# The expert layer of a two-layer block: the last 64 of 256 tokens by gathered expert rows, and the gates' one-hot rows by one comparison and ScalarE

## The chip, the cores and the metric

One core of a Trainium2 chip runs the whole program. The metric is device time in microseconds (us), the median of three runs; the profile shows one execution.

## The reference

256 tokens of width 2048 pass through a first layer (a convolution and a state-space branch, then a layer of experts) and a second one (a delta-rule block and a banded attention). The change touches the experts only: 16,384 experts of one neuron each, of which every token picks 128 (8 heads, 16 each).

```python
def block(xb):                       # PEER_TOKEN_BLOCK = 128 tokens; 8 heads, 2 x 128 keys
    q = (xb @ w_q).reshape(PEER_TOKEN_BLOCK, PEER_HEADS, 2, PEER_HALF)
    s = jnp.einsum('thcd,hcnd->thcn', q, sub_keys).astype(jnp.float32)
    s_top, i_top = lax.top_k(s, PEER_TOPK)
    cand = s_top[:, :, 0, :, None] + s_top[:, :, 1, None, :]
    cand_idx = i_top[:, :, 0, :, None] * PEER_KEYS + i_top[:, :, 1, None, :]
    ...
    best, pos = lax.top_k(cand, PEER_TOPK)
    expert = jnp.take_along_axis(cand_idx, pos, axis=-1)
    gates = jax.nn.softmax(best, axis=-1).astype(xb.dtype)
    u_sel = u_tab[expert]
    v_sel = v_tab[expert]
    act = jax.nn.gelu(jnp.einsum('td,thkd->thk', xb, u_sel))
    return jnp.einsum('thk,thkd->td', gates * act, v_sel)
```

## The kernel before

The kernel reads no expert row by its index. It computes all 16,384 activations of all 256 tokens and multiplies them by a dense matrix of gates, which is zero where an expert is not picked.

Every matrix product is made of split operands. A piece of weights of 128 x 1024 (512 KB) is fetched into one of three buffers `raw` (L150, the SP queue); ScalarE casts it to a rounded high part `wh` (L162), VectorE subtracts that from it and leaves the low part `wl` (L163). `wh` and `wl` are rings of 2048 columns. `self.width` says how many columns one cast and one subtraction take: 1024 (W1) in the mixers, 512 (W2) from the experts on. Both are put ahead of other work in the engines' programs (`high_priority`). The activations stand in the same two parts beside each other, so `dual` makes a product from two instructions: `wh` on both parts (512 columns, L175) and `wl` on the high part (256 columns, L176). `fold` adds the two halves of the result (ScalarE L181, VectorE L182).

The expert layer runs in this order:

- **Queries** (`experts_in`): 16 blocks of 16 products each with `peer_w_q`; each block's scores against the sub-keys go into a table, and VectorE picks the top 16 of them by `topk`, in small steps that are laid between the products (`Side`, `TSTEP` steps a block). These steps reach into the next stage.
- **peer_u**: 128 blocks, block c giving expert activations for all tokens: 16 products, `fold`, a scaling by `rstd` (L797), a gelu into `w` (L801). From c = 31 on, when the top-k is done, `gates` runs beside the products, `GRATE` steps for each product: for each token three VectorE comparisons with a counting row (L942, L944) make a one-hot row of the first key scaled by the gate's power of two, and two of the second key scaled by the gate's high and low part. After eight tokens 16 products (L954) give a 128 x 128 block of gates for each of them, and `gate_block` multiplies it into `w` (VectorE L966) where block c is done, or copies it there (ScalarE L968) where it is not. For tokens whose gates are there when a block is finished, gelu and gate are multiplied at once (L803, L804).
- **peer_v** (`experts_out`): `w` is the stationary operand now. It is split again, 128 experts x 256 tokens at a time (ScalarE L1009, VectorE L1010), and for each of the two halves of the tokens three products of 512 columns (L1018 to L1020) are added in PSUM. Three groups of 512 output columns are summed in one pass over the experts, the fourth in a second pass, beside which the first three are finished: transposed, added to the residual and prepared for the second layer (`finish`, `take_x2`).

Each engine works through its instructions in the order of its program.

Of the kernel before, what the change touches and what calls it, by code (L numbers as in the profile page):

```python
# [10 lines left out]
F32 = mybir.dt.float32  # L11
# [11 lines left out]
P = 128  # L23
W1 = 1024
W2 = 512
STEP = (6, 2, 2.25, 3.7, 3, 2)
GRATE = 0.2
# [18 lines left out]
KT = 16  # L46
MAGIC = 1.5 * 2.0**23
# [68 lines left out]

class K:
# [54 lines left out]
    def dual(self, pf, wh, wl, hl, start, stop):  # L172

        nc = self.nc
        nc.tensor.matmul(pf, lhsT=wh, rhs=hl, start=start, stop=False)  # L175
        return nc.tensor.matmul(pf[:, :T], lhsT=wl, rhs=hl[:, 0], start=False, stop=stop)  # L176

    def fold(self, pf):

        t = self.foldp.tile([P, T], F32, name="fold")[: pf.shape[0]]  # L180
        self.nc.scalar.copy(t, pf[:, T:])  # L181
        self.nc.vector.tensor_tensor(out=pf[:, :T], in0=pf[:, :T], in1=t, op=ALU.add)  # L182
        return pf[:, :T]

    def gemm_steps(self, ps, pieces, x):

        last = 8 * len(pieces) - 1
        k = 0
        for src in pieces:
            for wh, wl in self.load_split(src):  # L190
                self.marks["P"] = self.dual(ps, wh, wl, x.hl[:, k], k == 0, k == last)
                k += 1
                if k > last:
                    self.fold(ps)
                yield

    def gemm(self, pieces, x, between=None):
        pf = self.gps_tile()
        for _ in self.gemm_steps(pf, pieces, x):
            if between is not None:  # L200
                next(between, None)
        return pf[:, :T]
# [68 lines left out]
    def first(self):  # L271
        tc = self.tc
        self.width = W1
        with ExitStack() as ctx:
# [3 lines left out]
            with ExitStack() as c2:  # L278
# [6 lines left out]
                self.width = W2  # L285
                self.em = Tmp(E(tc.tile_pool(name="em", bufs=8)))
# [455 lines left out]
    def experts_in(self):  # L742
# [3 lines left out]
        with ExitStack() as ctx:  # L746
# [6 lines left out]
            ijg = c2.tile([P, 5, T], F32, name="ijg")  # L753
# [11 lines left out]
            nc.gpsimd.tensor_copy(iota16, iota)  # L765
            tk = self.topk(sc, bt, ijg, iota)
            def score(k, q):
# [8 lines left out]
            for k in range(16):  # L776
# [8 lines left out]
                side.step(TSTEP, (self, "V"))  # L785
            score(15, q)
            side.add(tk(8))

            w = [self.big_tile("w0").rearrange("p (c t) -> p c t", c=32)]
            tokens = Side()  # L790
            self.gated = 0

            for c in range(P):
                self.block = c
                ps = self.gemm([I["peer_u"][c, 0], I["peer_u"][c, 1]], x, self.mix((tokens, GRATE, "")))
                g = sm.tile([P, T], F32, name="gg")
                V.tensor_tensor(out=g, in0=ps, in1=rstd, op=ALU.mult)  # L797
                d = self.expert(w, c)
                n = self.gated
                if n < T:  # L800
# [5 lines left out]
                if c == 31:  # L806
                    side.drain()
                    w += [self.big_tile(f"w{k}").rearrange("p (c t) -> p c t", c=32) for k in (1, 2)]
                    w += [self.half_tile(f"w{k}").rearrange("p (c t) -> p c t", c=16) for k in (3, 4)]
                    tokens.add(self.gates(wps, ijg, iota16, w))  # L810
            assert not tokens.q
            self.w = w

    def expert(self, w, c):
        return w[c // 32][:, c % 32, :] if c < 96 else w[3 + (c - 96) // 16][:, c % 16, :]

    def topk(self, sc, bt, ijg, iota):
# [54 lines left out]
        def last():  # L872
# [39 lines left out]
            ij = ij.rearrange("p c h e k -> p c h (e k)")  # L912
            for h in range(2):
                for k, src in enumerate((ij[:, 0, h, :], ij[:, 1, h, :], ex.rearrange("p g k -> p (g k)")[:, h * P : h * P + P])):
                    pt = self.ips.tile([P, 512], F32, name="pt", tag="i")[:, :P]
                    nc.tensor.transpose(pt, src, self.ident)
                    nc.scalar.copy(ijg[:, k, h * P : h * P + P], pt)
# [5 lines left out]
            half = area(128).bitcast(F16)  # L923
# [7 lines left out]
    def gates(self, wps, ijg, iota, w):  # L931
# [6 lines left out]
        for t in range(T + GLAG):  # L938
            if t < T:
                oj = self.em.tile([P, 3, P], F16, name="oj")  # L940
                oi = oj[:, 2, :].bitcast(BF16)
                V.tensor_scalar(out=oi, in0=iota, scalar1=ijg[:, 0, t : t + 1], scalar2=ijg[:, 4, t : t + 1], op0=ALU.is_equal, op1=ALU.mult)  # L942
                for k in range(2):
# [822 lines left out]
```

## Time and profile before

| | |
|---|---|
| median of 3 runs | 3355.83 us (3353.45 to 3359.02) |
| the profiled execution's own time | 3351.08 us |
| its span, first to last instruction | 3349.3 us |
| mean granted TensorE clock | 0.996 of full speed |
| busy share: TensorE, VectorE, ScalarE, GpSimd | 98%, 80%, 60%, 5% |
| bytes moved | 584.49 MB, 175 GB/s on average |

A row of the trace gives an instruction's duration from its start to its end. Instructions of one engine can overlap, so a sum of durations can exceed the engine's busy time; TensorE's overlap most, and their pace is read from the starts. "DMA share" is the mean busy share of the core's 16 DMA engines.

### The profile page before, as it was taken

The numbers are of one execution on the slowest core, as the hardware profiler recorded it, in microseconds if no ns is written. First come the engines' busy times: TensorE is split into PE (matmuls) and PEld (weight loads), VectorE is DVE, ScalarE is ACT, GpSimd is POOL, SyncE is SP. The second block draws the span as 40 slices with busy tenths as digits, with TensorE's granted clock in tenths as the row PEclk, the third lists the DMA queues.
The fourth block names the chain that finished last, engine by engine and source line by source line (L and its number), as shares of the span: only waits on it lengthen the run. The fifth ranks groups of instructions, "written<-read, shape, count | busy, mean of one in ns | idle before, by whom it ended". The sixth has DMA issues, their size and how long they took to land.

```text
span 3349.3 us, 53879 instructions
## 1 busy us (share of the span) xinstructions
PE 3291.0 (98%) x17962; PEld 2780.5 (83%) x17962; DVE 2667.1 (80%) x6200; ACT 2021.3 (60%) x4529; POOL 171.6 (5%) x319
## 2 busy tenths in 40 slices
PE   8999999999999999999999999999999999999999
PEld 7787778888888888888888888778888888888888
DVE  8999987789999999996555556868888768666685
ACT  6577755555555555555555556767666666566664
POOL 1211110000000000000000000000222100000000
PEclk9999999999999999999999999999999999999999
DMA  6544345765556555555666666655443436655556
GB/s 210 160 143 139 133 127 188 216 193 178 187 183 179 180 177 182 177 182 183 193 194 195 193 192 198 209 183 171 143 138 117 145 105 211 198 177 176 173 171 181
DMA packets 167655, 584.49 MB, mean 175 GB/s; under 512 B 19184, under 2 KB 25616, under 8 KB 167120
## 3 DMA queue, kind: packets, MB, share of 16 engines
q1 hardware_dynamic: 165600, 574.94, 54.8%
q0 software_dynamic: 1776, 6.10, 0.6%
q8 instruction: 141, 2.31, 0.3%
q14 instruction: 138, 1.13, 0.1%
HBM read 573.88 MB, written 7.09 MB: 173 GB/s over the span
## 4 chain that ended last, share of the span: by engine, by line
PE 90%; DVE 5%; ACT 2%; issue 1%; DMA 1%; POOL 1%; SPq 0%; ACTq 0%; DVEq 0%; POOLq 0%
PE g L175 36%; PE g L176 18%; PE va L1018 7%; PE va L1019 7%; PE va L1020 7%; PE g L1609 3%; PE g L1610 3%; PE g L1608 3%; DVE wl L163 2%; PE ip L1345 1%; ACT wh L162 1%; PE yp L639 1%; PE wp L954 1%; PE cps L175 1%; PE bu L611 1%
## 5 line engine op out<-in xcount | busy, mean ns | idle before, releaser
L162 ACT CAST wh<-raw 128x512 fp32r<-128x512 f32 (+1 forms) x1920 | 1274.2, 664 | 1080.3 <-PE g L175 553.2
L163 DVE TENSOR_TENSOR wl<-raw,wh 128x512 fp32r<-128x512 f32 (+1 forms) x1920 | 1433.8, 748 | 589.6 <-ACT wh L162 571.8
L175 PE MATMUL g<-X,wh 128*128 128x512 f32 x4752 | 1707.7, 401 | 23.0 <-ACT wh L162 8.8
L176 PE MATMUL g<-X,wl 128*128 128x256 f32 x4752 | 1337.0, 281 | 2.3 <-DVE wl L163 2.2
L175 PEld LDWEIGHTS g<-X,wh 128*128 128x128 f32 x4752 | 894.3, 188 | 234.6 <-issue 10.8
L176 PEld LDWEIGHTS g<-X,wl 128*128 128x128 f32 x4752 | 898.0, 189 | 9.9 <-DVE wl L163 5.1
L1018 PE MATMUL va<-wh,ah 128*128 128x512 f32 x1024 | 398.4, 391 | 4.5 <-DVE gg L797 2.3
L1019 PE MATMUL va<-wh,al 128*128 128x512 f32 x1024 | 400.2, 391 | 0.3 <-DVE al L1010 0.3
L1020 PE MATMUL va<-wl,ah 128*128 128x512 f32 x1024 | 399.1, 390 | 0.0
L1018 PEld LDWEIGHTS va<-wh,ah 128*128 128x128 f32 x1024 | 191.7, 188 | 46.9 <-ACT ah L1009 7.5
L1019 PEld LDWEIGHTS va<-wh,al 128*128 128x128 f32 x1024 | 192.6, 188 | 43.3 <-DVE al L1010 3.3
L1020 PEld LDWEIGHTS va<-wl,ah 128*128 128x128 f32 x1024 | 192.7, 188 | 39.7
L175 PE MATMUL g<-xo,wh 128*128 128x512 f32 x512 | 179.6, 395 | 0.0
L182 DVE TENSOR_TENSOR g<-g,fold 128x256 f32<-128x256 f32 x377 | 159.8, 424 | 4.5 <-ACT fold L181 4.0
L1608 PE MATMUL g<-wh,X 128*128 128x512 f32 x384 | 151.9, 396 | 0.0
L1610 PE MATMUL g<-wl,X 128*128 128x512 f32 x384 | 150.5, 392 | 0.0
L1609 PE MATMUL g<-wh,X 128*128 128x512 f32 x384 | 150.1, 391 | 0.0
L181 ACT COPY fold<-g 128x256 f32<-128x256 f32 x377 | 138.2, 367 | 13.5 <-DVE g L182 7.7
L176 PE MATMUL g<-xo,wl 128*128 128x256 f32 x512 | 143.6, 280 | 0.0
L944 DVE TENSOR_SCALAR oj<-iota,ijg 128x128 f16<-128x128 f16 x512 | 142.6, 307 | 0.0
L175 PEld LDWEIGHTS g<-xo,wh 128*128 128x128 f32 x512 | 96.0, 187 | 22.8 <-DVE xo L1471 0.3
L1010 DVE TENSOR_TENSOR al<-w,ah 128x256 fp32r<-128x256 f32 x256 | 106.7, 418 | 0.9 <-ACT ah L1009 0.8
(478 smaller groups left out, 3577.0 us busy)
## 6 DMA issues: line engine op xcount, KB each, us to landing
raw<-peer_u SPq DMA_DIRECT2D x256, 512.0 KB, 3.5
raw<-peer_v SPq DMA_DIRECT2D x256, 512.0 KB, 3.5
raw<-a_w_in SPq DMA_DIRECT2D x128, 512.0 KB, 3.5
raw<-w_in SPq DMA_DIRECT2D x112, 512.0 KB, 3.5
raw<-b_w_t SPq DMA_DIRECT2D x96, 512.0 KB, 3.5
raw<-w_out SPq DMA_DIRECT2D x32, 512.0 KB, 4.3
raw<-peer_w_q SPq DMA_DIRECT2D x32, 512.0 KB, 3.5
raw<-a_w_out SPq DMA_DIRECT2D x32, 512.0 KB, 3.7
```

Of the source, the lines that this page charges most:

```text
L162: self.marks["A"] = nc.scalar.copy(wh[:, e], raw[:, e])
L163: self.marks["V"] = nc.vector.tensor_tensor(out=wl[:, e], in0=raw[:, e], in1=wh[:, e].bitcast(F32), op=ALU.subtract)
L175: nc.tensor.matmul(pf, lhsT=wh, rhs=hl, start=start, stop=False)
L176: return nc.tensor.matmul(pf[:, :T], lhsT=wl, rhs=hl[:, 0], start=False, stop=stop)
L182: self.nc.vector.tensor_tensor(out=pf[:, :T], in0=pf[:, :T], in1=t, op=ALU.add)
L944: V.tensor_scalar(out=oj[:, k, :], in0=iota, scalar1=ijg[:, 1, t : t + 1], scalar2=ijg[:, 2 + k, t : t + 1], op0=ALU.is_equal, op1=ALU.mult)
L1018: nc.tensor.matmul(ps, lhsT=ah, rhs=wh, start=first, stop=False)
L1019: nc.tensor.matmul(ps, lhsT=al, rhs=wh, start=False, stop=False)
L1020: nc.tensor.matmul(ps, lhsT=ah, rhs=wl, start=False, stop=last)
L1608: nc.tensor.matmul(ps[a], lhsT=xh[:, k, s], rhs=wh, start=k == 0, stop=False)
L1609: nc.tensor.matmul(ps[a], lhsT=xl[:, k, s], rhs=wh, start=False, stop=False)
L1610: self.marks["P"] = nc.tensor.matmul(ps[a], lhsT=xh[:, k, s], rhs=wl, start=False, stop=k == KT - 1)
```

## The change

The last 64 tokens (S) no longer take part in the products of peer_u: those, the one-hot rows and the gates are made for 192 tokens (N). For the 64, a class `Picks` holds the picked experts' numbers and gates with one row for each token and half of its 128 picks. Gather c brings pick c of each row, 128 expert rows, into one of two buffers by an indirect DMA from GpSimd's queue. In peer_u there are 64 gathers of rows of 2048 elements (8 KB each), and one VectorE instruction for each multiplies the rows by the tokens and sums them (`dots`, two steps for three blocks, from c = 32 on). In peer_v there are 64 gathers of 1536 and then 64 of 512 elements, and VectorE adds each, times its coefficient, to a sum (`sums`, one step for two blocks); `finish` folds the two rows of a token by a product with `sel`. In peer_v the first operand now has tokens 64 to 191 and needs three products as before; the second has the high and low part of tokens 0 to 63 side by side and needs two.

The one-hot rows of two tokens are made by one VectorE comparison of 512 elements, and ScalarE scales them by the gates in six instructions of 128 elements. `self.width` is not lowered to 512 any more, the pool `em` has 7 buffers in place of 8, `w` lies in blocks of 42, and `GRATE` goes from 0.2 to 0.08, each step now being two tokens. Three copies of the expert tables in row order are added to the kernel's inputs.

```diff
-GRATE = 0.2
+GRATE = 0.08
+S = 64
+N = T - S
+NW = 8192 // N
+USTEP = 2.0 / 3.0
...
+class Picks:
...
+    def rows(self, x, rstd):
+        k, nc = self.k, self.k.nc
+        xs = self.buf[0].rearrange("p (k i t) -> p k i t", k=KT, i=2)
+        h, l = (v.bitcast(F32)[:, :, N:].unsqueeze(2).to_broadcast([P, KT, 2, S]) for v in x)
+        nc.vector.tensor_tensor(out=xs, in0=h, in1=l, op=ALU.add)
+        r = rstd[:, N:].unsqueeze(1).unsqueeze(1).to_broadcast([P, KT, 2, S])
+        nc.vector.tensor_tensor(out=xs, in0=xs, in1=r, op=ALU.mult)
...
+                nc.tensor.transpose(ps[:, i * P : i * P + P], xs[:, 4 * q + i, :], k.ident)
+            nc.scalar.copy(self.acc[:, 512 * q : 512 * q + 512], ps)
...
+    def gather(self, table, c, w):
+        b = self.buf[c % 2][:, :w]
+        off = bass.IndirectOffsetOnAxis(ap=self.idx[:, c : c + 1], axis=0)
+        self.k.nc.gpsimd.indirect_dma_start(out=b, out_offset=None, in_=table, in_offset=off)
+        return b
+    def stream(self, table, w, use):
+        bufs = [self.gather(table, c, w) for c in range(2)]
+        yield
+        for c in range(S):
+            use(c, bufs[c % 2])
+            if c + 2 < S:
+                self.gather(table, c + 2, w)
+            yield
+    def dots(self):
...
+            V.tensor_tensor_reduce(out=b, in0=b, in1=self.acc, scale=1.0, scalar=0.0, op0=ALU.mult, op1=ALU.add, accum_out=self.h[:, c : c + 1])
...
+    def sums(self, table, o, w):
...
+                V.scalar_tensor_tensor(out=acc, in0=b, scalar=s, in1=acc, op0=ALU.mult, op1=ALU.add)
...
     def dual(self, pf, wh, wl, hl, start, stop):
...
+        n = hl.shape[2]
+        nc.tensor.matmul(pf[:, : 2 * n], lhsT=wh, rhs=hl, start=start, stop=False)
+        return nc.tensor.matmul(pf[:, :n], lhsT=wl, rhs=hl[:, 0], start=False, stop=stop)
...
-                self.width = W2
-                self.em = Tmp(E(tc.tile_pool(name="em", bufs=8)))
+                self.em = Tmp(E(tc.tile_pool(name="em", bufs=7)))
...
+                if k == 1:
+                    self.picks.rows(x, rstd)
...
-                ps = self.gemm([I["peer_u"][c, 0], I["peer_u"][c, 1]], x, self.mix((tokens, GRATE, "")))
+                ps = self.gemm([I["peer_u"][c, 0], I["peer_u"][c, 1]], x, self.mix((tokens, GRATE, ""), (sparse, USTEP / 16, "")), N)
...
+            sparse.drain()
...
-                V.tensor_scalar(out=oi, in0=iota, scalar1=ijg[:, 0, t : t + 1], scalar2=ijg[:, 4, t : t + 1], op0=ALU.is_equal, op1=ALU.mult)
-                for k in range(2):
-                    V.tensor_scalar(out=oj[:, k, :], in0=iota, scalar1=ijg[:, 1, t : t + 1], scalar2=ijg[:, 2 + k, t : t + 1], op0=ALU.is_equal, op1=ALU.mult)
+        for t in range(0, N + GLAG, 2):
...
+                V.tensor_tensor(out=oj[:, :, 0::2, :], in0=iota.unsqueeze(1).unsqueeze(1).to_broadcast([P, 2, 2, P]),
+                                in1=self.ij16[:, t : t + 2, :].unsqueeze(3).to_broadcast([P, 2, 2, P]), op=ALU.is_equal)
+                for i in range(2):
+                    c = slice(t + i, t + i + 1)
+                    oi = oj[:, i, 0, :]
+                    nc.scalar.activation(oi.bitcast(BF16), oi, AF.Copy, scale=ijg[:, 4, c])
+                    nc.scalar.activation(oj[:, i, 1, :], oj[:, i, 2, :], AF.Copy, scale=ijg[:, 3, c])
+                    nc.scalar.activation(oj[:, i, 2, :], oj[:, i, 2, :], AF.Copy, scale=ijg[:, 2, c])
...
+                        pa = self.em.tile([P, 2 * N + S], F32R, name=f"pa{e}")
+                            nc.scalar.copy(pa[:, :N], a)
+                            nc.scalar.copy(pa[:, N:T], a[:, :S])
+                            V.tensor_tensor(out=pa[:, T:], in0=a, in1=pa[:, :N].bitcast(F32), op=ALU.subtract)
+                        parts.append((pa[:, S:N], pa[:, T + S :], pa[:, N:T], pa[:, N : T + S]))
...
-                                nc.tensor.matmul(ps, lhsT=ah, rhs=wh, start=first, stop=False)
-                                nc.tensor.matmul(ps, lhsT=al, rhs=wh, start=False, stop=False)
-                                nc.tensor.matmul(ps, lhsT=ah, rhs=wl, start=False, stop=last)
+                            nc.tensor.matmul(a, lhsT=ah, rhs=wh, start=first, stop=False)
+                            nc.tensor.matmul(a, lhsT=al, rhs=wh, start=False, stop=False)
+                            nc.tensor.matmul(a, lhsT=ah, rhs=wl, start=False, stop=last)
...
+                            nc.tensor.matmul(b, lhsT=bhl, rhs=wh, start=first, stop=last)
+                            if not last:
+                                nc.tensor.matmul(b[:S], lhsT=bh, rhs=wl, start=False, stop=False)
                     side.step()
+                    sparse.step()
+                sparse.drain()
```

## Rows read from the trace of the kernel before

**Rows 1.** Windows by stage: us, busy PE PEld DVE ACT POOL, clock, DMA share, GB/s.
```profile
682.00:777.00 95.00, 95.00 (x565) 83.61 (x564) 82.89 (x264) 50.32 (x100) 0.84 (x2) 1.00 0.59 184
777.00:965.00 188.00, 188.00 (x1071) 163.16 (x1070) 178.63 (x481) 105.24 (x201) 0.00 (x0) 1.00 0.60 185
965.00:1525.00 560.00, 559.97 (x3564) 489.27 (x3563) 527.16 (x1532) 321.88 (x759) 0.00 (x0) 1.00 0.57 179
1525.00:2060.00 535.00, 532.74 (x2357) 441.15 (x2356) 316.27 (x530) 285.94 (x529) 0.00 (x0) 1.00 0.61 192
2060.00:2240.00 180.00, 177.51 (x778) 142.35 (x777) 143.90 (x292) 135.31 (x308) 2.82 (x10) 1.00 0.65 203
```

**Rows 2.** Timeline of TensorE in peer_u: start us, us, engine, line, operation.
```profile
1003.25 0.40 PE L175 MATMUL g<-X,wh 128*128 128x512 f32 x1
1003.48 0.28 PE L176 MATMUL g<-X,wl 128*128 128x256 f32 x1
1003.60 0.39 PE L175 MATMUL g<-X,wh 128*128 128x512 f32 x1
```

**Rows 3.** Timeline of TensorE in peer_v.
```profile
1700.28 0.39 PE L1018 MATMUL va<-wh,ah 128*128 128x512 f32 x1
...
1700.96 0.39 PE L1018 MATMUL va<-wh,ah 128*128 128x512 f32 x1
```

**Rows 4.** Groups of VectorE, 975 to 1520: count, busy us, mean ns, idle before.
```profile
L163 DVE TENSOR_TENSOR wl<-raw,wh 128x512 fp32r<-128x512 f32 x371 | 254.7, 686 | 21.3 <-ACT wh L162 19.7
L944 DVE TENSOR_SCALAR oj<-iota,ijg 128x128 f16<-128x128 f16 x512 | 142.6, 307 | 0.0
L942 DVE TENSOR_SCALAR oj<-iota,ijg 128x128 bf16<-128x128 f16 x256 | 78.5, 307 | 3.1 <-PE wp L954 2.8
L182 DVE TENSOR_TENSOR g<-g,fold 128x256 f32<-128x256 f32 x93 | 39.5, 424 | 0.0
L797 DVE TENSOR_TENSOR gg<-g,rstd 128x256 f32<-128x256 f32 x93 | 38.9, 419 | 2.7 <-PE wp L954 1.8
L966 DVE TENSOR_TENSOR w<-w,wp 128x256 f32<-128x256 f32 (+15 forms) x99 | 34.1, 356 | 0.0
L804 DVE TENSOR_TENSOR w<-w,gg 128x8 f32<-128x8 f32 (+31 forms) x89 | 25.5, 287 | 0.0
```

**Rows 5.** Windows, 975 to 1520 us, columns as in rows 1.
```profile
975.00:1520.00 545.00, 545.00 (x3480) 476.92 (x3479) 517.78 (x1516) 313.01 (x739) 0.00 (x0) 1.00 0.57 179
```

**Rows 6.** Groups of the whole run, shapes kept apart.
```profile
L163 DVE TENSOR_TENSOR wl<-raw,wh 128x1024 fp32r<-128x1024 f32 x192 | 238.5, 1242 | 66.4 <-ACT wh L162 66.1
L162 ACT CAST wh<-raw 128x1024 fp32r<-128x1024 f32 x192 | 201.0, 1047 | 161.6 <-PE g L175 147.0 <-issue 13.8
...
L1010 DVE TENSOR_TENSOR al<-w,ah 128x256 fp32r<-128x256 f32 x256 | 106.7, 418 | 0.9 <-ACT ah L1009 0.8
...
L674 DVE SCALAR_TENSOR_TENSOR cw<-cw 128x256 f32<-128x256 f32 x150 | 73.9, 534 | 0.0
```

**Rows 7.** Windows, 200 to 300 us, in the mixers, columns as in rows 1.
```profile
200.00:300.00 100.00, 98.42 (x536) 81.08 (x534) 99.91 (x181) 75.56 (x173) 10.31 (x12) 1.00 0.44 144
```

**Rows 8.** Timeline, two ScalarE scalings by a column of scales.
```profile
701.54 0.69 ACT L248 ACTIVATE dg<-ident,r_yi 128x128 f32<-128x128 f32 x2
```

**Rows 9.** Windows, 2294 to 2302 us, columns as in rows 1.
```profile
2294.00:2302.00 8.00, 8.00 (x48) 6.97 (x47) 6.71 (x16) 3.79 (x8) 0.20 (x2) 1.00 0.95 357
```

**Rows 10.** Timelines of GpSimd and VectorE, near 2291 and near 2388 us.
```profile
2291.53 0.56 POOL L1191 DMA_DIRECT2D rep<-gd  x1 [0.35 <-issue]
...
2291.99 0.69 DVE L163 TENSOR_TENSOR wl<-raw,wh 128x512 fp32r<-128x512 f32 x1 [0.69 <-ACT wh L162]
...
2388.18 3.81 POOL L1337 TENSOR_TENSOR xx<-tab 128x2048 f32<-128x2048 f32 x1 [2.92 <-DMA tab<-xdr]
...
2388.71 3.43 DVE L1268 TENSOR_SCALAR ksq<-ksq 128x2 f32<-128x2 f32 x1
```

**Rows 11.** Timeline of TensorE, products of full precision.
```profile
704.29 0.71 PE L770 MATMUL pq<-bs,q 128*128 128x128 f32 x4
```

More of the change, by code (lines that the diff above doesn't have):

```diff
@@ L174, in dual, with fold, gemm_steps @@
         nc = self.nc
[L175 to L185, printed above, removed]
+        n = hl.shape[2]
+        nc.tensor.matmul(pf[:, : 2 * n], lhsT=wh, rhs=hl, start=start, stop=False)
+        return nc.tensor.matmul(pf[:, :n], lhsT=wl, rhs=hl[:, 0], start=False, stop=stop)
+    def fold(self, pf, n=T):
+        t = self.foldp.tile([P, T], F32, name="fold")[: pf.shape[0], :n]
+        self.nc.scalar.copy(t, pf[:, n : 2 * n])
+        self.nc.vector.tensor_tensor(out=pf[:, :n], in0=pf[:, :n], in1=t, op=ALU.add)
+        return pf[:, :n]
+    def gemm_steps(self, ps, pieces, x, n=T):
         last = 8 * len(pieces) - 1
@@ L794, in experts_in @@
                 self.block = c
-                ps = self.gemm([I["peer_u"][c, 0], I["peer_u"][c, 1]], x, self.mix((tokens, GRATE, "")))
-                g = sm.tile([P, T], F32, name="gg")
-                V.tensor_tensor(out=g, in0=ps, in1=rstd, op=ALU.mult)
+                ps = self.gemm([I["peer_u"][c, 0], I["peer_u"][c, 1]], x, self.mix((tokens, GRATE, ""), (sparse, USTEP / 16, "")), N)
+                g = sm.tile([P, N], F32, name="gg")
+                V.tensor_tensor(out=g, in0=ps, in1=rstd[:, :N], op=ALU.mult)
+                if c == 31:
+                    side.drain()
+                    w += [self.big_tile(f"w{k}")[:, : NW * N].rearrange("p (c t) -> p c t", t=N) for k in (1, 2)]
+                    w.append(self.picks.rest)
+                    tokens.add(self.gates(wps, ijg, iota16, w))
+                    sparse.add(self.picks.dots())
                 d = self.expert(w, c)
                 n = self.gated
-                if n < T:
+                if n < N:
                     nc.scalar.activation(d[:, n:], g[:, n:], AF.Gelu_apprx_tanh)
@@ L805, in experts_in @@
                 side.step(TSTEP, (self, "V"))
[L806 to L810, printed above, removed]
             assert not tokens.q
+            sparse.drain()
             self.w = w
     def expert(self, w, c):
-        return w[c // 32][:, c % 32, :] if c < 96 else w[3 + (c - 96) // 16][:, c % 16, :]
+        return w[c // NW][:, c % NW, :]
     def topk(self, sc, bt, ijg, iota):
@@ L912, in last @@
             ij = ij.rearrange("p c h e k -> p c h (e k)")
+            self.picks.take(ij[:, :, 1, :], ex.rearrange("p g k -> p (g k)")[:, P:], area(P), area(P), area(P))
+            yield
             for h in range(2):
```

127 lines of the change are left out of this document (89 added, 38 removed).

## The prediction

> **What bounds the kernel now.** I read the busy time by stage first, to see which engine is full where; then the timeline of TensorE inside one block, for the price of a column; then the groups of instructions of the stage, for the prices on the other engines. The change touches five stages, one after the other in [rows 1]: the queries (682 to 777 us), peer_u while the top-k is worked out (to 965), peer_u while the gates are made (to 1525), peer_v for three column groups (to 2060), and peer_v for the fourth (to 2240). In all of them TensorE is busy to 98% or more, and the reader should look at the column beside it: VectorE has 178.63 of 188 us and 527.16 of 560 in the two halves of peer_u (95 and 94%), but 316.27 of 535 in the long half of peer_v (59%).
>
> TensorE is at its pace. In a peer_u block a 512-column product starts 0.23 us before the next instruction and the 256-column product 0.12 us before the one after; a pair takes 0.345 us, 0.449 ns a column, and the pairs follow without a gap [rows 2]. In peer_v three products of 512 columns take 0.68 us from one start to its like, so 0.227 us each [rows 3]. So fewer columns are worth time only until VectorE, with 5% to spare in peer_u, is full.
>
> **What goes from TensorE.** A peer_u pair falls from 768 to 576 columns: at 0.449 ns, 0.259 us. A block of 16 pairs goes from 5.53 to 4.14 us; the gate products fall from 512 to 384 with the tokens. If TensorE alone counted, 128 blocks would give 177 us. In peer_v five products replace six: 512 fewer at 0.227 us, 116 us. So at most 290 us. Neither the trace nor the code before has a 192-column product in this format; I price it by the column and keep the other possibility as a rival.
>
> **VectorE in peer_u with gates.** Rows overlap: in 975 to 1520 us the VectorE rows of [rows 4] sum to 613.8 us, against 517.78 busy over 1,516 instructions [rows 5]. One instruction behind another therefore costs its mean less 0.063 us. Widths are priced by the slope of one form: a subtraction wl takes 686 ns at 512 columns [rows 4] and 1242 at 1024 [rows 6], 1.086 ns a column. For the 96 blocks after c = 31:
>
> - wl, now 1024 wide since the width is no longer lowered: 192 x (1.242 - 0.063) = 226 us.
> - The fold and the scaling by rstd at 192 columns: 192 x (0.42 - 0.07 - 0.063) = 56 us.
> - The product with the gelu and the gate products: 25.5 + 34.1 us less overlap, by 192/256: 36 us.
> - One-hot rows: 96 comparisons of 512 elements in place of 768 of 128. The trace has no such comparison; the bounds are 0.307 us (a row of 128 elements) and 0.686 (a tensor pair of 512). Two tensor operands put it nearest the second: 96 x 0.623 = 60 us.
> - The new dot products: 64 of 2048 elements. By the slope 1.242 + 1024 x 1.086 ns = 2.35 us; 64 x 2.29 = 147 us.
>
> The sum is 525 us. The stage has 527.16 now. So what the one-hot rows free (768 x 0.244 = 187 us) the dots and the rest take again, and VectorE, not TensorE (96 x 4.14 = 398 us and the gate products), becomes the bound of the stage. How full can it run? Where the mixers use the same 1024-wide ring it is busy 99.91 of 100 us [rows 7], against 94% in this stage now; I take 96.5%, as ScalarE is also loaded: 544 us, 16 less than 560.
>
> ScalarE takes 576 scalings. Two of the like shape take 0.69 us together [rows 8], so 0.29 to 0.35 each: 167 to 202 us. From 321.88 us [rows 1] it goes to 489 to 524 of 544, before the little that wider casts and narrower rows give back. It stays off the bound, but the cast wh, on which wl waits, now stands behind up to six scalings, about 2 us.
>
> DMA: 96 blocks bring 100.7 MB and 64 gathers of 128 rows of 8 KB 67.1 MB: 168 MB, 308 GB/s over 544 us. The trace shows 357 GB/s at a share of 0.95 [rows 9], so the transfers would need some 470 us. They fit, and two gathers in flight have about 17 us for a turn.
>
> **The other stages.** Peer_u without gates: VectorE's top-k stays. The wider wl gives 64 x (2 x 0.623 - 1.179) = 4 us, the narrower fold and scaling 64 x 0.07 = 4; the address arithmetic costs 1. 178.63 becomes 171, at 96.5% 177: 11 less than 188, I take 10.
>
> Queries: the token rows cost two VectorE instructions of 2048 elements (4.6 us) and 16 transposes; wl gives 2 back: +3 us.
>
> Peer_v, three groups: TensorE needs 64 x 30 x 0.227 = 435 us against 64 x 36 x 0.227 = 523 before. VectorE per pair of blocks: 3 x 1.18 + 2 x (0.418 - 0.07 - 0.063) + the sum step of 1536. The nearest row for that is wl plus the difference of L674 to L1010 at 256 columns (534 - 418 ns) [rows 6]: 1.242 + 0.556 + 0.116 = 1.91, less overlap 1.85 us. In all 5.96 of 6.81 us. But the ring now has two halves: a piece is used by ten products (2.27 us), then cast (1.05) and subtracted (1.24) [rows 6] before it can be used again. Two pieces share that turn, (2.27 + 1.05 + 1.24) / 2 = 2.28 us, so nothing is left over when wl waits behind a sum step. The ends are none of it late, 438 us, and all of it, 438 + 64 x 1.85 = 556. I take half: 497, 38 less than the 535; with the rounding of the ends, 40 less.
>
> Peer_v, fourth group: TensorE needs 64 x 10 x 0.227 = 145 us. VectorE has 143.90 now; less 4 for wl and 9 for the narrower al, and 64 sum steps of 512 elements at 0.74 us add 47: 178, at 96.5% 184 against 180: +5. Draining the last dot and sum steps at three stage ends: 2.3 + 1.9 + 0.7, +5.
>
> Gathers: 192 on GpSimd. Below, 0: the start of one transfer on GpSimd takes 0.56 us and the subtraction beside its end 0.69, as elsewhere [rows 10]. Above, those 0.56 us each, if VectorE stands all the while. The row of the subtraction is the nearest; I take 0 and keep 192 x 0.56 = 108 us for the range.
>
> Sum: 3 - 10 - 16 - 40 + 5 + 5 = -53 us. From the profiled execution's own 3351.08 us, 3298; the median is 4.75 above it, so 3303 us, 1.6% faster.
>
> [...] [Rows 10] also show an instruction of two columns on VectorE that takes 3.43 us, beside a GpSimd instruction of 3.81 us that ends 0.15 us before it. [...]
>
> **Rivals.**
>
> - *Gathers hold VectorE* (the other side). Place: every gather's issue on GpSimd, in three stages where VectorE is full or feeds the ring. For: the 3.43 us in [rows 10]. Against: the 0.69 us there. At 0.56 us each, 108 us: 3411 us. It decides from 53 / 192 = 0.28 us a gather.
> - *The ring and ScalarE's queue stall TensorE.* For: no slack in the turn above, six scalings ahead of a cast. Against: [rows 7]. Peer_u with gates 580, peer_v 556, fourth group 195: 3 + 20 + 21 + 15 + 5 = +64, 3420 us; half of it ends near 3390.
> - *VectorE has more room.* One-hots at 0.31 us (96 x 0.37 less), full use, no late wl: 3 - 15 - 71 - 97 + 0 + 3 = -177, 3179 us. For: 99.91 in [rows 7]. Against: 94% in this very stage.
> - *The 192-column product is not priced by the column.* Two full-precision products of 128 columns stand in the trace as four passes and take 0.71 us [rows 11]; without the last's 0.275 us of latency they start 0.145 us apart, 2.27 ns a column. At that rate 192 columns take 0.44 us; with loads 0.11 apart (a quarter less), 0.33. With the lower, a pair takes 0.173 + 0.33 = 0.50 us, 2048 pairs 1030: peer_u 1052 against 748, and +304 + 3 - 40 + 10 = +277, 3633 us. For: nothing narrower than 256 stands in this format. Against: 512 and 256 columns go at one price [rows 2].
>
> **How the numbers follow.** Chances: the forecast 0.49, gathers 0.13, stalls 0.18, more room 0.10, the narrow product 0.10. The time is the forecast's, 3303. The range leaves out the narrow product, the lower half of more room and the worst of gathers: 3220 to 3420. A measurement tells 0.2% (7 us) from no change. Faster: the forecast and more room, and stalls and gathers where they come out small (0.05): 0.64. Within 0.2%: 0.06, out of stalls and gathers. Slower: 0.30. The forecast's own range is 3240 to 3345.
>
> **What would show it.** Right: peer_u pairs start 0.26 us apart but with gaps; VectorE at 95% or more in peer_u, TensorE's gaps there ended by wl; peer_v for three groups near 495 us; the fourth no shorter than 180. Wrong: dots far from 2.3 us or comparisons far from 0.65; VectorE instructions stretched beside gathers; a VectorE idle on gathers; pairs at 0.45 us or more without gaps.

## The result, and the profile after

The changed kernel takes 3669.1 us (median of 4 runs, 3668.23 to 3670.69); the kernel before, run beside it, 3357.4 us. The ratio is 1.0929, interval 1.091 to 1.0948. The forecast was 3303 us, range 3220 to 3420: wrong in sign, by 366 us.

Windows by stage of the changed kernel, in the columns of [rows 1] (queries; peer_u with the top-k; peer_u with gates; peer_v, three groups; peer_v, fourth group):

```profile
682.00:780.00 98.00, 98.00 (x582) 85.35 (x581) 84.22 (x234) 46.94 (x74) 0.53 (x2) 1.00 0.56 175
780.00:968.00 188.00, 164.63 (x1070) 155.41 (x1069) 170.99 (x419) 89.44 (x135) 1.64 (x3) 0.99 0.59 184
968.00:1922.00 954.00, 649.84 (x3440) 593.22 (x3439) 674.55 (x886) 443.55 (x1118) 286.83 (x194) 0.80 0.70 246
1922.00:2390.00 468.00, 462.92 (x2014) 354.02 (x2014) 283.18 (x346) 273.09 (x481) 0.00 (x0) 1.00 0.70 224
2390.00:2560.00 170.00, 158.58 (x677) 117.25 (x675) 126.45 (x229) 137.34 (x368) 2.71 (x10) 0.96 0.69 216
```

The whole loss lies in one stage, peer_u with gates: 954 us in place of 560. Both stages of peer_v are shorter than before (468 for 535, 170 for 180). And in the long stage no engine is full: VectorE 71%, TensorE 68%, ScalarE 46%, the transfers 70%. A stage in which nothing is full is one in which the engines wait for each other, so the next view is that of the waits, from 968 to 1922 us (who waited for what: us in total, times, longest):

```profile
ACT w L909 <- DVE gg L899: 398.4, 94, 11.1
PE g L273 <- DVE wl L259: 284.6, 139, 8.3
POOL sb L174 <- DVE sa L208: 180.6, 70, 4.6
DVE sa L208 <- DMA sb<-v_b,sa: 83.2, 37, 5.0
DVE sb L191 <- DMA sb<-u_rows,sa: 79.4, 52, 7.6
DVE sa L208 <- DMA sb<-v_a,sa: 62.2, 40, 3.2
```

VectorE stands 225 us for gathered rows (the last three lines), TensorE 285 us for wl, and ScalarE 398 us, in front of a gelu, for gg. The surprise is v_a and v_b: the sum steps, written in peer_v, run here. The groups of the same window, shapes kept apart, have all of them, and the prices (L191 is the dot product, L208 the sum step, L1049 the comparison, L1054 one of the scalings):

```profile
L259 DVE TENSOR_TENSOR wl<-raw,wh 128x1024 fp32r<-128x1024 f32 x191 | 233.2, 1221 | 51.6 <-ACT wh L258 51.4
L191 DVE CUSTOM_DVE_ANT_0 sb<-sb,sa 128x2048 f32<-128x2048 f32 x64 | 146.6, 2291 | 79.4 <-DMA sb<-u_rows,sa 79.4
L208 DVE SCALAR_TENSOR_TENSOR sa<-sb,sa 128x1536 f32<-128x1536 f32 x63 | 114.5, 1817 | 62.3 <-DMA sb<-v_a,sa 62.2
L1054 ACT ACTIVATE oj<-oj,sa 128x128 bf16<-128x128 f16 x192 | 75.9, 396 | 27.1 <-DVE oj L1049 20.4
L1049 DVE TENSOR_TENSOR oj<-iota,ij 128x512 f16<-128x512 f16 x96 | 65.1, 684 | 0.0
L208 DVE SCALAR_TENSOR_TENSOR sa<-sb,sa 128x512 f32<-128x512 f32 x63 | 47.2, 750 | 83.3 <-DMA sb<-v_b,sa 83.2
```

A dot product takes 2.29 us (2.35 priced), a comparison 0.684 (0.686), a sum step 1.82 (1.91): the prices held. Without the sum steps (161.7 us), VectorE's work in the stage is 513 us, against 525 in the prediction. What a wait costs is seen in the timeline of VectorE, with the TensorE instruction that ends a gap:

```profile
1301.66 2.29 DVE L191 CUSTOM_DVE_ANT_0 sb<-sb,sa 128x2048 f32<-128x2048 f32 x1 [1.84 <-DMA sb<-u_rows,sa]
1303.88 1.22 DVE L259 TENSOR_TENSOR wl<-raw,wh 128x1024 fp32r<-128x1024 f32 x1
1305.01 0.35 DVE L899 TENSOR_TENSOR gg<-g,rstd 128x192 f32<-128x192 f32 x1
...
1307.51 2.29 DVE L191 CUSTOM_DVE_ANT_0 sb<-sb,sa 128x2048 f32<-128x2048 f32 x1 [1.40 <-DMA sb<-u_rows,sa]
1309.73 1.22 DVE L259 TENSOR_TENSOR wl<-raw,wh 128x1024 fp32r<-128x1024 f32 x1
...
1305.15 0.36 PE L273 MATMUL g<-X,wl 128*128 128x192 f32 x1 [2.97 <-DVE wl L259]
```

A dot stands here between any two wl, 5.9 us from the last, where the step in the code asks for two dots in three blocks. It waits 1.84 us for its rows; the wl behind it waits with it, though its cast (1.03 us from 1297.23, on ScalarE) had ended at 1298.26, and TensorE stands 2.97 us for that wl. Behind the wl come gg (the scaling by `rstd`), the gelu, and behind the gelu on ScalarE the next cast.

The products, in the timeline of TensorE where weights are ready (beside [rows 2]):

```profile
850.74 0.36 PE L272 MATMUL g<-X,wh 128*128 128x384 f32 x1
850.94 0.25 PE L273 MATMUL g<-X,wl 128*128 128x192 f32 x1
851.02 0.36 PE L272 MATMUL g<-X,wh 128*128 128x384 f32 x1
851.22 0.25 PE L273 MATMUL g<-X,wl 128*128 128x192 f32 x1
851.31 0.36 PE L272 MATMUL g<-X,wh 128*128 128x384 f32 x1
...
2000.01 0.39 PE L1131 MATMUL va<-wh,pa 128*128 128x512 f32 x1
...
2001.16 0.39 PE L1131 MATMUL va<-wh,pa 128*128 128x512 f32 x1
```

Pairs start 0.285 us apart, not 0.259. In peer_v (the last two lines) five products take 1.15 us from one start to its like, 0.23 each as forecast (beside [rows 3]).

### The profile page after: what moved, and what is told of

The parts are those of the page before. It is cut to its first block, busy times and chain, and to the rows that moved or that the text cites. A ratio compares the mean times of both kernels' runs of the same rounds, so it can differ in the third digit from the quotient of the medians.

```text
span 3666.8 us, 50106 instructions
## 1 busy us (share of the span) xinstructions
PE 3267.2 (89%) x17386; PEld 2760.7 (75%) x17386; DVE 2719.0 (74%) x4887; ACT 2055.2 (56%) x4477; POOL 460.3 (13%) x516
## 4 chain that ended last, share of the span: by engine, by line
PE 41%; DVE 4%; ACT 3%; DMA 2%; issue 1%; ACTq 0%; SPq 0%; DVEq 0%
PE g L272 10%; PE g L273 5%; PE va L1133 3%; PE va L1132 3%; PE va L1138 3%; PE va L1136 3%; PE va L1131 3%; PE g L1730 2%; PE g L1728 2%; PE g L1729 2%; DVE wl L259 2%; ACT wh L258 2%; PE ip L1465 1%; DMA raw<-peer_v 1%; PE ip L1510 0%
## 5 line engine op out<-in xcount | busy, mean ns | idle before, releaser
L272 PE MATMUL g<-X,wh 128*128 128x512 f32 (+1 forms) x4752 | 1726.1, 410 | 43.4 <-ACT wh L258 28.1
L259 DVE TENSOR_TENSOR wl<-raw,wh 128x1024 fp32r<-128x1024 f32 x1056 | 1299.9, 1232 | 605.5 <-ACT wh L258 595.9
L273 PE MATMUL g<-X,wl 128*128 128x256 f32 (+1 forms) x4752 | 1361.5, 287 | 316.3 <-DVE wl L259 315.5
L258 ACT CAST wh<-raw 128x1024 fp32r<-128x1024 f32 x1056 | 1107.2, 1049 | 849.5 <-PE g L272 445.0
L208 DVE SCALAR_TENSOR_TENSOR sa<-sb,sa 128x1536 f32<-128x1536 f32 (+1 forms) x126 | 161.7, 1284 | 145.6 <-DMA sb<-v_b,sa 83.2
L1131 PE MATMUL va<-wh,pa 128*128 128x512 f32 x512 | 202.1, 395 | 10.3 <-ACT pa L1122 5.6
L1133 PE MATMUL va<-wl,pa 128*128 128x512 f32 x512 | 205.0, 400 | 2.0 <-DVE wl L259 1.9
L1132 PE MATMUL va<-wh,pa 128*128 128x512 f32 x512 | 205.1, 401 | 0.9 <-DVE pa L1124 0.8
L191 DVE CUSTOM_DVE_ANT_0 sb<-sb,sa 128x2048 f32<-128x2048 f32 x64 | 146.6, 2291 | 79.4 <-DMA sb<-u_rows,sa 79.4
L1138 PE MATMUL va<-wl,pa 128*64 128x512 f32 x508 | 202.7, 399 | 0.0
L1136 PE MATMUL va<-wh,pa 128*128 128x512 f32 x512 | 200.8, 392 | 0.0
L279 DVE TENSOR_TENSOR g<-g,fold 128x256 f32<-128x256 f32 (+1 forms) x377 | 152.0, 403 | 3.5 <-ACT fold L278 3.4
```

What stands on the lines that cost most here:

```text
L258: self.marks["A"] = nc.scalar.copy(wh[:, e], raw[:, e])
L259: self.marks["V"] = nc.vector.tensor_tensor(out=wl[:, e], in0=raw[:, e], in1=wh[:, e].bitcast(F32), op=ALU.subtract)
L272: nc.tensor.matmul(pf[:, : 2 * n], lhsT=wh, rhs=hl, start=start, stop=False)
L273: return nc.tensor.matmul(pf[:, :n], lhsT=wl, rhs=hl[:, 0], start=False, stop=stop)
L1131: nc.tensor.matmul(a, lhsT=ah, rhs=wh, start=first, stop=False)
L1132: nc.tensor.matmul(a, lhsT=al, rhs=wh, start=False, stop=False)
```

## The experiments

The theory: the planner that orders each engine's instructions brought dots and sums ahead of their place, faster than their rows land ("early order"). Rivals: the two-part ring and ScalarE's queue hold TensorE in any order; the gathers cost time wherever they stand; the narrow products. Each run below was timed once, and is set against one run of the kernel before on the same chip. These four runs of before gave 3349.85 to 3362.00 us, so a difference under some 12 us is taken as none. "peer_u" and "peer_v" are the time from the first fetch of their weights to the last (745 and 707 us before, 1139 and 620 after).

| run | over before, us | peer_u | peer_v |
|---|---|---|---|
| the change | +311.7 | 1139 | 620 |
| e1 hold | +183.8 | 876 | 724 |
| e2 hold, 512 wide | +118.9 | 839 | 697 |
| e3 hold, no gathers | +65.2 | 881 | 625 |
| e4 no dots, sums, gathers | +2.2 | 830 | 614 |
| e5 e4, 512 wide | -99.2 | 737 | 612 |
| e6 e4, one-hot rows as before | -91.4 | 745 | 611 |
| e7 e4, gelu later | +1.5 | 838 | 612 |
| e8 before, 1024 wide | +9.2 | 745 | 712 |
| e9 e4, gelu later still | +14.8 | 845 | 613 |
| e10 hold, narrow v rows | +120.2 | 876 | 661 |
| e11 the change, 512 wide | +257.6 | 1089 | 614 |
| e12 e2, gelu later still | +125.2 | 854 | 691 |
| e13 e4, gelu and scalings later | -78.6 | 761 | 614 |
| e14 e2, gelu and scalings later | +86.1 | 810 | 707 |
| e15 before, new one-hot rows | +12.1 | 754 | 714 |
| e16 e4, both e5 and e6 | -139.7 | 698 | 613 |

**The order (e1, e2, e11).** The held run orders dots and sums on VectorE behind the last wl written before them:

```diff
-... (sparse, USTEP / 16, "")), N)
+... (sparse, USTEP / 16, "V")), N)
 ...
-                    sparse.step()
+                    sparse.step(1, (self, "V"))
```

> Every dot product and every sum step is ordered behind the subtraction wl of the place where it is written: one dot per three pieces of weights in place of one per piece, the sum steps one per two blocks of peer_v in place of inside peer_u. Early-order theory (VectorE's program brings dots and sums forward faster than the gathers land, and the wl behind them waits): the stage of peer_u with gates falls from 957 us to 545-600, peer_v for three groups goes up to 470-530, in all 3290-3430 us. Ring theory (two halves of the ring and the gelu ahead of the next cast hold TensorE whatever the order): peer_u stays above 850, in all 3600 or more. Gather theory (each of the 192 gathers costs VectorE time wherever it stands): peer_u with gates above 700, in all 3480 or more.

3533.61 us: between the theories. The early order is worth 128 us (+311.7 to +183.8), but peer_u stays at 876, far from the forecast's 719 (745 less 26), and peer_v is now longer than before.

Casts and subtractions of 512 added to it:

> As the run with dots and sums held in place, and the casts and subtractions 512 wide again as in the kernel before, so four parts of the ring turn in place of two. Early-order theory: within 60 us of the held run, on either side (256 more starts of VectorE instructions in peer_u at about 0.13 us against a finer ring). Ring theory: at least 150 us less than the held run, since the ring was the cause.

3468.75 us, 65 less: beyond the 60 of the one theory, far from the 150 of the other. It is a gain, but not the cause.

The same width in the change itself, with its early order (`self.width = W2` alone):

> The changed kernel with one edit: casts and subtractions 512 wide. With dots and sums held, that edit gave 65 us (3534 to 3469). If the early order and the ring are separate causes, it gives about the same here: 3560-3640. If the early order only hurts through the two-part ring, four parts take it away: 3470-3540. If the early order alone sets the time: 3655 or more.

3608.87 us, 54 less than the change, each against its own before: about what the width gives with the order held, as two separate causes would have it.

**The gathers (e3, e10).** First no transfer at all, with the same instructions on VectorE:

```diff
-        self.k.nc.gpsimd.indirect_dma_start(out=b, out_offset=None, in_=table, in_offset=off)
 ...
-            V.tensor_tensor_reduce(out=b, in0=b, in1=self.acc, ...)
+            V.tensor_tensor_reduce(out=b, in0=self.acc, in1=self.acc, ...)
```

> As the held run, with all 192 indirect transfers left out: the dots and sums work on one buffer that was set to zero and on the accumulator, so the 64 tokens' expert terms are not computed, while VectorE does the same instructions. Gather theory: 100 us or more under the held run. Early-order theory: within 20 us of it, since with dots 8 us apart the gathers land in time.

3415.02 us, 119 less than held, so the number is what the gather theory said. But its place is not: peer_u is the same (881 and 876), and VectorE is busy 517.5 and 517.8 of 693 us there, with 2.282 us for a dot in both and 1.225 and 1.224 for a wl, the middle of the whole run. 99 of the 119 us lie in peer_v (724 and 625), and most of the rest, 17.5 us, behind its last fetch. Windows of peer_v for three groups, first held, then without gathers:

```profile
1680.00:2197.00 517.00, 476.45 (x1933) 338.64 (x1934) 375.24 (x390) 252.92 (x455) 77.24 (x63) 0.98 0.84 290
```

```profile
1680.00:2131.00 451.00, 449.05 (x1930) 337.08 (x1930) 373.08 (x385) 259.82 (x451) 0.00 (x0) 1.00 0.67 224
```

VectorE does the same 63 sum steps in both. What differs is the transfers, 84% of the time at 290 GB/s against 67%, and in the waits of the whole run the casts stood 146.2 us for raw from peer_v when held:

```profile
ACT wh L258 <- DMA raw<-peer_v: 146.2, 61, 5.8
```

and 36.5 us without gathers. Whether it is bytes or the number of gathers was tried with v_b's rows of 512 in place of v_a's:

```diff
-        yield from self.stream(table, w, use)
+        yield from self.stream(self.k.I["v_b"], 512, lambda c, b: use(c, self.buf[c % 2][:, :w]))
```

> As the held run (3534 us), but the 64 gathers for the three column groups bring rows of 512 elements in place of 1536, while the sum steps still work on 1536 (two thirds of them on old data, so these columns are wrong for the 64 tokens). Traffic theory (in peer_v the gathers take transfer time from the fetches of weights): peer_v for three groups falls from 517 to 450-485 us, in all 3465-3505. Start theory (each gather costs its start on GpSimd, whatever it brings): within 12 us of 3534. VectorE theory (the sum steps themselves are the cost): within 12 us of 3534.

3471.49 us, 62 less (63.5 by the chips' own runs of before), the stage 454 us in place of 517. Same number of gathers, same sum steps, a third of the bytes: in this stage it was traffic.

**What is left without sparse work (e4).** Dots, sums and gathers are left out:

```diff
-                    sparse.add(self.picks.dots())
 ...
-                sparse.add(picks.sums(I["v_a" if g0 == 0 else "v_b"], 512 * g0, 512 * ng))
```

> The changed kernel without its dot products, sum steps and their gathers: the expert terms of the last 64 tokens are left out. Narrow-product theory (the pair of 384 and 192 columns costs 0.285 us, not 0.259): TensorE bounds peer_u with gates at 96 x 16 x 0.285 = 438 us and some 40 for the gate products, 470-500 us; peer_v 440-460 and 150-165; in all 3130-3210 us. Ring theory: peer_u with gates stays above 650 us with nothing to wait for but the ring, in all above 3350. If scalings on ScalarE hold the stage, peer_u with gates 520-600 with ScalarE above 90 per cent.

3352.01 us: no gain at all over the kernel before, with a quarter fewer columns on TensorE in peer_u and no dots or sums on VectorE. Peer_v is near what the narrow-product theory said (448 and 164 us, TensorE busy 447.73 and 156.37 of them). Peer_u with gates is not: it takes 647 us, and the whole is at the ring theory's number (above 3350), while ScalarE is at 69%, not above 90 (to the first product of peer_v the stage has 661 us, the 660 of two expectations below). The stage, in the columns of [rows 1]:

```profile
965.00:1612.00 647.00, 535.43 (x3455) 485.71 (x3454) 390.73 (x631) 444.08 (x1117) 1.03 (x2) 0.96 0.46 156
```

The timeline of ScalarE there shows why:

```profile
1302.07 1.03 ACT L258 CAST wh<-raw 128x1024 fp32r<-128x1024 f32 x1
1303.00 0.31 ACT L278 COPY fold<-g 128x192 f32<-128x192 f32 x1
1305.05 0.28 ACT L908 ACTIVATE w<-gg 128x96 f32<-128x96 f32 x1 [1.74 <-DVE gg L899]
1305.24 0.27 ACT L910 ACTIVATE gg<-gg 128x96 f32<-128x96 f32 x1
1305.65 0.40 ACT L1053 ACTIVATE oj<-oj,sa 128x128 bf16<-128x128 f16 x1
1305.96 0.39 ACT L1054 ACTIVATE oj<-oj,sa 128x128 f16<-128x128 f16 x1
1306.25 1.03 ACT L258 CAST wh<-raw 128x1024 fp32r<-128x1024 f32 x1
...
1308.51 1.03 ACT L258 CAST wh<-raw 128x1024 fp32r<-128x1024 f32 x1
1309.45 0.31 ACT L278 COPY fold<-g 128x192 f32<-128x192 f32 x1
1311.50 0.28 ACT L908 ACTIVATE w<-gg 128x96 f32<-128x96 f32 x1 [1.74 <-DVE gg L899]
```

and the waits of TensorE in the same stretch:

```profile
1307.34 0.44 PE L272 MATMUL g<-X,wh 128*128 128x384 f32 x1 [0.58 <-ACT wh L258]
1308.60 0.36 PE L273 MATMUL g<-X,wl 128*128 128x192 f32 x1 [0.82 <-DVE wl L259]
```

A block takes 6.45 us (1305.05 to 1311.50; that is also the middle value of the whole stage, from one fold copy to the next), where sixteen pairs need 4.56. It is a closed chain: cast, then on VectorE wl, the fold and gg behind it, then on ScalarE the gelu, two scalings, the next cast, four more scalings, and the cast with which it began. ScalarE is idle 1.74 us in this block in front of the gelu (162.2 us over 94 such waits in the stage), while the cast behind it could go: the half that it fills was read for the last time near 1303.8, and it starts at 1306.25. In these rows ScalarE takes its queue in order.

With the whole work held (e1) a dot joins this chain, on VectorE between the fold and gg, with the gelu behind it:

```profile
1304.44 0.36 DVE L279 TENSOR_TENSOR g<-g,fold 128x192 f32<-128x192 f32 x1
1304.71 2.28 DVE L191 CUSTOM_DVE_ANT_0 sb<-sb,sa 128x2048 f32<-128x2048 f32 x1
1306.92 0.35 DVE L899 TENSOR_TENSOR gg<-g,rstd 128x192 f32<-128x192 f32 x1
...
1307.31 0.29 ACT L909 ACTIVATE w<-gg 128x104 f32<-128x104 f32 x1 [1.63 <-DVE gg L899]
```

The dot waits for no rows here. From one fold copy to the next, the middle value over the stage's blocks is 7.51 us, against 6.45 in e4.

**The chain's links (e5, e6, e8, e15, e16).** Two of the links come from the change: casts and subtractions of 1024, and the scalings. Each was undone alone, then both:

```diff
+                self.width = W2
                 self.em = Tmp(E(tc.tile_pool(name="em", bufs=7)))
```

> The changed kernel without dots, sum steps and gathers (the last 64 tokens' expert terms are left out), and with casts and subtractions 512 wide. The run without them at 1024 wide took 3352 us, 660 of it in peer_u with gates, where TensorE needs about 460. Chain theory (one block after the other in a closed chain: the subtraction, the fold and the gg behind it on VectorE, the gelu, the scalings, then the next cast behind them on ScalarE): half a cast and half a subtraction less, some 1 us a block of it, so 70-110 us less: 3240-3285. Scalings theory (ScalarE's own work is too much): 10 us or less gained, since the starts cost ScalarE more: 3340 or more.

3255.9 us, peer_u 737: the chain theory's number. A ring of four parts would help against the ring too; the next run leaves it at two.

```diff
-                V.tensor_tensor(out=oj[:, :, 0::2, :], in0=iota..., in1=self.ij16..., op=ALU.is_equal)
-                for i in range(2):
-                    ...
+                for i in range(2):
+                    V.tensor_scalar(out=oi, in0=iota, scalar1=ijg[:, 0, c], scalar2=ijg[:, 4, c], op0=ALU.is_equal, op1=ALU.mult)
+                    for k in range(2):
+                        V.tensor_scalar(out=oj[:, k, :], in0=iota, scalar1=ijg[:, 1, c], scalar2=ijg[:, 2 + k, c], ...)
```

> The changed kernel without dots, sum steps and gathers (the last 64 tokens' expert terms are left out), with the one-hot rows made as before, three comparisons with a factor for each token on VectorE and nothing on ScalarE; casts 1024 wide. Scalings theory: the chain loses some 1.8 us of scalings on ScalarE a block and VectorE gets 0.8 us: peer_u with gates 500-570, in all 3200-3270 us. If the width is the cause: within 40 us of 3352.

3263.67 us, with 576 instructions on VectorE in place of 96 comparisons. VectorE has more to do (452 us in a stage of 561, against 391 of 647 in e4), and the kernel is faster, since the scalings left the chain on ScalarE. The ring still has two parts.

> The changed kernel without dots, sum steps and gathers (the last 64 tokens' expert terms are left out), with the one-hot rows made on VectorE as before and casts 512 wide. Each edit alone gave 90-96 us (3264 and 3256, from 3352). If both are links of one chain that still sets the block: both together 3190-3225, and TensorE at 0.285 us a pair (some 480 us with the gate products) becomes the bound of peer_u with gates. If either one alone already opens the chain: within 15 us of 3256.

3222.3 us: both count, though not in full (142 less than e4 together, 101 and 94 alone, each against its own before), and peer_u with gates is 514 us, with TensorE busy 474 of them.

> The kernel before with one edit: casts and subtractions stay 1024 wide through peer_u and peer_v, as in the changed kernel. Width theory: a two-part ring alone makes TensorE wait, peer_u with gates 600 or more in place of 560, in all 3390 or more. Chain theory: with 256 tokens TensorE has 5.53 us a block to hide the chain in and there are no scalings on ScalarE, so 3340-3385, most of it in peer_u.

3364.34 us, 9 over its own before, within the noise, peer_u unchanged at 745 (the edit is that `self.width = W2` is left out of the kernel before).

> The kernel before with the second half of the change alone: one comparison for two tokens on VectorE, six scalings on ScalarE, for all 256 tokens; no gathers, casts 512 wide. ScalarE theory: 768 scalings at 0.3 us bring its 322 us in peer_u with gates to 550 of 560, so it becomes the bound there: 580-620 us, in all 3370-3420. If its queue has room enough beside a TensorE at 5.53 us a block: 3340-3360.

3374.12 us: the total lies in the ScalarE theory's range, but it is only 12 us over its own before, at the edge of the noise, and the stage with gates takes 567 us, not 580 to 620, although ScalarE is busy 189.37 of 200 us there (1200 to 1400 us). (The edit also takes `GRATE` to 0.11, gives the pool `em` 5 buffers and makes the gate products in fours in place of eights.) So neither half of the change costs more than some 12 us while TensorE needs 5.53 us a block. Together, under a TensorE that needs a block every 4.56 us, they are links of the chain that sets the block.

**Opening the chain (e7, e9, e12, e13, e14).** These leave width and scalings alone and order the gelu behind a later cast on ScalarE: its calls, with the product behind them, go into a function that is called so many pairs later (9, then 17), behind the cast last written (mark "A").

```diff
-                d = self.expert(w, c)
-                n = self.gated
-                ...
+                def gelu(c=c, g=g):
+                    ...
+                    self.block = c + 1
+                late.add(gelu)
 ...
+... self.mix((late, 9, "A"), (tokens, GRATE, ""), ...
```

> The changed kernel without dots, sum steps and gathers (the last 64 tokens' expert terms are left out), with each block's gelu and its product ordered behind the cast of the second piece of the next block instead of ahead of it; nothing else changed. Chain theory: the cast no longer waits for the gelu's input (1.74 us of idle time on ScalarE in a block of 6.45), peer_u with gates falls from 660 to 530-590, in all 3220-3280 us. Ring theory (a half of the ring comes free too late, whatever stands ahead of the cast): within 30 us of 3352.

3356.59 us, a run that tested nothing: in its timeline the gelu stands where it stood, since the cast chosen already ran ahead of it.

> The changed kernel without dots, sum steps and gathers (the last 64 tokens' expert terms are left out), with each block's gelu ordered one cast later than in the run before it: behind the cast of the first piece of the block after the next, which is the cast that stood behind it. Chain theory: that cast no longer waits for the gelu's input, but two scalings that wait for a comparison still stand ahead of it; 40-120 us under 3352: 3230-3310. If the scalings take the gelu's place in the chain entirely: within 15 us of 3352. Ring theory: within 15 us of 3352, with casts that wait for TensorE in the place of gelus that wait for gg.

3366.07 us. The gelu moved, and the scalings took its place (170.4 us of waits for a comparison in the stage, where the gelus of e4 had 162.2):

```profile
1303.78 0.31 ACT L303 COPY fold<-g 128x192 f32<-128x192 f32 x1
1304.03 0.54 ACT L1108 COPY w<-wp 128x48 f32<-128x48 f32 x2
1304.45 0.19 ACT L1108 COPY sa<-wp 128x16 f32<-128x16 f32 x1
1306.50 0.40 ACT L1083 ACTIVATE oj<-oj,sa 128x128 bf16<-128x128 f16 x1 [1.85 <-DVE oj L1078]
1306.81 0.39 ACT L1084 ACTIVATE oj<-oj,sa 128x128 f16<-128x128 f16 x1
1307.10 1.03 ACT L283 CAST wh<-raw 128x1024 fp32r<-128x1024 f32 x1
```

> Dots and sums held, casts 512 wide, and each block's gelu ordered behind the first cast of the block after the next. Chain theory: 20-80 us less than the same without the last edit (3469): 3390-3450. If VectorE's work with the dots (160 of 200 us there) is what is left: within 15 us of 3469.

3476.46 us, no gain. Here the edit hardly changed the wait: the gelus stand 127.1 us for gg in the stage, 133.5 without the edit (e2).

For e13 the scalings are written one step after their comparison as well, and ordered behind the last cast. The edit, of which the order is shown, also makes the gate products in fours in place of eights and a step later (`GLAG` 4), and takes `GRATE` to 0.085; no run has these alone:

```diff
-... self.mix((late, 17, "A"), (tokens, GRATE, ""), ...
+... self.mix((late, 17, "A"), (tokens, GRATE, "A"), ...
 ...
+            for oj, c in pend:
+                ... the six scalings of the pair of tokens compared one step ago
```

> The changed kernel without dots, sum steps and gathers (the last 64 tokens' expert terms are left out), 1024 wide; gelus ordered behind the cast that stood behind them, and scalings too: they are written one step after their comparison and ordered behind the last cast, so that no instruction that waits for VectorE's end of a block stands ahead of that cast. Chain theory: now the chain is open, peer_u with gates falls from 647 to 530-580 us, in all 3235-3290. Ring theory: the cast waits for TensorE to free its half instead; within 20 us of 3352.

3283.44 us, 81 less than e4 (each against its own before), peer_u 761, the stage 577 in place of 647. The ring has two parts as before, and the waits in front of a cast fell: 13.4 us for gelus (162.2 in e4) and 42.6 for scalings. With e6 this speaks for the chain against the ring. The ring is not out of it: with the chain opened, casts wait 47.5 us for TensorE (17.5 in e4).

> The whole work, with dots and sums held, casts 512 wide, and gelus and scalings behind the cast that stood behind them. Chain theory: 30-80 us under the run without the last edit (3469): 3390-3440, since VectorE with the dots needs some 545 us of peer_u with gates and transfers hold peer_v at some 500 and 200. VectorE theory (its queue with the dots in it sets the pace, whatever ScalarE does): within 15 us of 3469.

3448.11 us, between the two theories: 33 less than without that edit when each is set against its own before, 21 less by the bare times. It has e13's side edits too. It is the shortest run with the whole work, still 86 over the kernel before, which no version with the whole work beats.

## Why the prediction was wrong

From the kernel before to the changed one, step by step: e4 +2, dots and sums on VectorE in their place +63 (e3), gathers +119 (e1), early order +128. The sum took the first for a gain, had the second as work on VectorE that fits, and the last two at nothing.

- *What goes from TensorE: at most 290 us.* Near in peer_v (448 and 164 us in e4, without sum steps; 435 and 145 priced). In peer_u the pair was priced by the column, 0.259 us; it takes 0.285. That makes 128 blocks 53 us longer than priced. The rival of 0.50 us a pair was far off.
- *VectorE in peer_u with gates: 525 us of work at 96.5% full, 544 us.* **This is the step that failed.** The work was right (513; 518 when held), the fullness wrong: 71% in the change, 75% held. The 99.91% of [rows 7] came from the mixers, another stage, and proved nothing for this one. What bounds the stage is a chain over two engines' queues, and its length was never added up: two casts, six scalings, two gelus, the fold, and the idle 1.74 us in front of the gelu make 6.45 us a block against TensorE's 4.56. The prediction saw the link ("the cast wh, on which wl waits, now stands behind up to six scalings, about 2 us") and costed it at nothing.
- *Peer_u without gates: -10.* The same step failed in small: VectorE's work was right (170.99 us; 171 priced), its share was 91% and not 96.5, and the stage takes 188 us as before.
- *They fit, and two gathers in flight have about 17 us for a turn.* That was the code's rate, two dots for three blocks. On VectorE the order is the planner's, and nothing held them: one after almost every wl, 5.9 us apart in the rows above, while u_rows land 7.2 us (the median; 6.3 over all gathers) after their start. VectorE waited 225 us for rows, those of the sums included, which is one of the prediction's own signs of being wrong.
- *Peer_v, three groups: 497.* The sum steps ran in peer_u instead, so the 468 us of the change are no test of it, nor its 170 of the 185 for the fourth group. When held in peer_v, ring stalls proved small, 451 us without gathers against the end of 438 with none late; but transfers, which were worked out for peer_u only, add 66 us (517), and the fourth group takes 205 us with them, 169 without. Both peer_v stages need 201 MB with gathers (134 MB of weights, 67 MB of rows).
- *Draining: +5.* Unnoticed in the change, where the sums were long done. When held, the fourth group's last gather is started at 2417 us, 26 us after the last fetch of weights.
- *Queries +3.* The first fetch of peer_u is at 780.6 us, 3.7 later.
- *Gathers hold VectorE* (rival, 0.13). No: in peer_u VectorE is busy 517.8 us with gathers and 517.5 without, and a wl, beside which such starts can fall, takes 1.224 us with them and 1.225 without, the middle of the whole run. The start on GpSimd takes 0.94 to 2.0 us there, far from the 0.56 of [rows 10], and costs peer_u nothing (876 and 881 us). Whether a start waits for VectorE is not shown.
- *The ring and ScalarE's queue stall TensorE* (rival, 0.18). The right mechanism, with ScalarE's queue and not the ring in it, priced at +64 us; the chain alone took what TensorE gave up, and the early order came on top.

What stays open: how much of the 128 us of early order is waiting for rows and how much is the lower granted clock. It was 0.80 over the long stage in the change and 0.96 held. In the change, behind the gap of 2.97 us shown above, the granted clock is 0.50 from 1305.7 to 1307.2 us and pairs start 0.53 us apart; in e4, in the block after the gaps shown above, they start 0.53 us apart from 1309.9 to 1313 us. Open too is what sets the pace of e14: its stage with gates takes 627 us, with TensorE busy 85%, VectorE 83% and the transfers 76%.

## What to carry to other kernels

Before taking work from the bound engine, add up the chain that one iteration closes over the queues of the others, waits included (6.45 us a block in e4, against TensorE's 4.56); its length, and not any engine's share of busy time, can be the next bound, and moving work to an engine that looks idle can lengthen it (here the scalings, 94 us by e4 and e6). A rate in the code is no order: work that nothing pins lands where the planner has room, and a wait for a transfer in it holds what stands behind (above, a dot waited 1.84 us for its rows, and TensorE 2.97 us for the wl behind it). Count the bytes of every stage that a transfer can land in, not only of the first.

## What was not expected of the hardware

- A 192-column product behind a 384-column one, each with its own load of 128 columns, takes 0.085 us and the pair 0.285, 0.495 ns a column, where 512 and 256 columns go at 0.449 [rows 2].
- An indirect transfer of 128 rows keeps GpSimd for 0.94 us at least, 1.68 in the middle for u_rows in the change; VectorE's wl takes 1.224 us with such starts (e1) and 1.225 without (e3), the middle of the whole run.
- Gathers of 6 KB rows beside a stream of 512 KB fetches took the transfers to 84% of the time at 290 GB/s, and the stage took 517 us in place of 451; at 75% and 259 GB/s (rows of 2 KB) it took 454.
